# Three pairs of each output projection as seven products of quarters, with sums of the merged values

## The chip, the cores and the metric
The kernel runs on one core of a Trainium2 chip. The core has four compute engines with their own instruction queues: TensorE (PE, matmuls; PEld are its weight loads), VectorE (DVE), ScalarE (ACT) and GpSimd (POOL). SyncE (SP) and POOL issue most DMA transfers. Each queue runs in its own fixed order, and an instruction that waits for a semaphore holds up all that stand behind it. The metric is device microseconds of one execution, as a median of several.

## The reference, cut to what matters
Two layers over 512 tokens of 1024 channels. Each layer normalizes x, projects it, runs three token mixers, merges their gated outputs and adds one output projection to the residual. A final RMSNorm follows.

```
for layer in range(2):
    ...
    merged = (sigmoid(ga) * (ya @ w_br_a[layer])
              + sigmoid(gb) * (yb @ w_br_b[layer])
              + sigmoid(gc) * (yc @ w_br_c[layer]))
    x = x + merged @ w_out[layer]
return rmsnorm(x, final_norm_g)
```

All is float32. The kernel keeps that precision by splitting each operand into a high part (rounded to the matmul's format, `fp32r`) and a low part (the rest), and by three matmuls for each product: high x high, high x low, low x high (`mm3`, lines 130 to 132).

## The kernel before, in words
Channels lie on partitions, so x is eight tiles of 128 x 512 (channels x tokens). T0 and T1 are the first and the last 256 tokens. An output projection has eight units of 128 output channels. A unit reads two weight blocks of 128 x 512 (four blocks of 128 input channels each) and all eight merged tiles, high and low (`st["MH", i]`, `st["ML", i]`).

**Layer 0** (`o_item`, line 769 on): 24 matmuls of 512 columns per unit, then VectorE adds the residual out of PSUM (L782), SP stores the new x to DRAM (`x1d`), ScalarE and VectorE split it for layer 1 (L156, L159), and the squares are summed on POOL. After each unit one `v_item` of layer 1 runs (12 matmuls of 512 columns).

**Layer 1** (`last_item`, line 801 on): the units run twice, once for T0 and once for T1, 24 matmuls of 256 columns each, so that the final norm of the first half can be computed and stored while the second half is multiplied. VectorE adds the residual (L821) and sums squares (L832); ScalarE squares and scales.

**Weights.** `load` issues the transfers ahead of use, and `split_to` makes the high and low parts. Most blocks go the DMA way: POOL loads the block into the high place, ScalarE writes its negative (L1139), and POOL loads the block once more on top of it, adding (L1140). Blocks of layer 1's output projection go the raw way: SP loads them, ScalarE casts the high part (L1133), VectorE or POOL subtracts (L1135).

**The gates.** The merge gates of most units are already computed in pairs by `pair_steps`: a product of two units, seen as two by two quarters (unit x half of the input channels, against tokens T0 and T1), takes seven products of quarters instead of eight. Three of the seven weight operands are blocks as they are (forms 0, 1, 4); four are differences of blocks (forms 2, 3, 5, 6; L1119), made on VectorE from raw blocks. The token sides are the inputs themselves or four sums per pair of input blocks (`sums`, L603 to L611; `sum_places` names the tiles that keep them).

**What sets the order.** In layer 0 a scheduler orders the instructions of each queue; `urgent` raises a priority. From the last gate pair of layer 1 on the program is under `manual_schedule`: each queue has the order in which the code is written. Either way the order is fixed before the run. PSUM has banks of the kinds `mm` (3), `att` (4) and `pv` (1).

Of the kernel before, what the change touches and what calls it, by code (L numbers as in the profile page):

```python
# [13 lines left out]
P = 128  # L14
# [50 lines left out]
def tile_trunk(ctx: ExitStack, tc: tile.TileContext, xT, wpk, gT, gfT, bfg, snk,  # L65
# [21 lines left out]
    def pv_bank():  # L87
        return PS("pv", 1)
# [73 lines left out]
    def square_sum(x, k):  # L162
        if k == 0:
            st["acc"] = T([P, S], F32, "ys", 2)
            nc.scalar.activation(st["acc"], x, AF.Square)
        else:
            sq = tmp()
            nc.scalar.activation(sq, x, AF.Square)
            eng = nc.vector if k == KT - 1 else nc.gpsimd
            eng.tensor_tensor(st["acc"], st["acc"], sq, op=ALU.add)  # L170

    def rms_pe(_, tbs=range(4), accs=("acc",)):
        ps = st["ss"] = pv_bank()
# [423 lines left out]
    def sums(l, k):  # L597
        def run():
            a, b = st["xa", k], st["xa", k + 4]
            for kk, t in ((k, a), (k + 4, b)):  # L600
                nc.scalar.activation(t, t, AF.Copy, scale=g_sb[:, l, kk:kk + 1])
            u, v = tmp(), tmp()
            nc.vector.tensor_tensor(u[:, T0], a[:, T1], b[:, T1], op=ALU.add)  # L603
            nc.vector.tensor_tensor(u[:, T1], u[:, T0], a[:, T0], op=ALU.subtract)
            nc.vector.tensor_tensor(v[:, T0], a[:, T0], a[:, T1], op=ALU.subtract)
            nc.vector.tensor_tensor(v[:, T1], b[:, T0], u[:, T1], op=ALU.subtract)
            h, lo = sum_places(k)
            for n, w in ((0, u), (1, v)):
                c = slice(n * S, n * S + S)
                nc.scalar.copy(h[:, c], w)  # L610
                nc.vector.tensor_tensor(lo[:, c], w, rd(h[:, c]), op=ALU.subtract)  # L611
            st["SH", k], st["SL", k] = h, lo
        return run

# [31 lines left out]
    def pair_steps(l, br, i, last=False):  # L646
# [5 lines left out]

        def A(half, tok):
            return lambda k: (XH[k + 4 * half][:, tok], XL[k + 4 * half][:, tok])

        def Sm(m):
            c = slice((m - 1) * HT, m * HT)
            return lambda k: (st["SH", k][:, c], st["SL", k][:, c])

        def prod(bank, form, xf):  # L660
            def pe(HL):
                new = bank not in d
                if new:
                    d[bank] = att_bank()[:, :HT]
                wh, wl = HL[0]
                for k in range(4):
                    c = slice(k * P, (k + 1) * P)
                    xh, xl = xf(k)
                    mm3(d[bank], wh[:, c], wl[:, c], xh, xl, new and k == 0, k == 3,
                        bank != "c")  # L670
            step(pe, [("w", l, br, i, form)])
# [77 lines left out]
        prod("b", 2, Sm(1))  # L749
        do(now(e5))  # L750
        prod("a", 3, Sm(2))
# [4 lines left out]
        prod("b", 4, Sm(4))  # L756
        do(now(c12))
        prod("a", 5, Sm(3))
# [12 lines left out]
    def o_item(e):  # L771
        d = {}

        def pe(HL):
            if e == 0:
                load_res(0)
                load_res(1)
            d["ps"] = run_unit(HL, [st["MH", i] for i in range(8)], [st["ML", i] for i in range(8)], LATE)

        def post():  # L780
            x1 = tmp()
            nc.vector.tensor_tensor(x1, d["ps"], st["xr", e], op=ALU.add)  # L782
            if e + 2 < 8:
                load_res(e + 2)
            nc.sync.dma_start(x1d[:, e, :], x1)
            split_x(x1, 1, e)
            square_sum(x1, e)
        step(pe, [("o", 0, e, h) for h in range(2)])
        do(post)

    def load_half(n):
        hf, e = divmod(n, 8)
        t = st["xr", n] = T([P, S], F32, "sz", 2)[:, :HT]
        nc.sync.dma_start(t, x1d[:, e, hf * HT:(hf + 1) * HT])

    def last_item(hf, e):
        d = {}
        n = 8 * hf + e  # L800
        tok = slice(hf * HT, (hf + 1) * HT)

        def pe(HL):
            if n == 0:
                load_half(0)
                load_half(1)
            if hf == 0:
                st["WO", e] = HL
            ps = mm_bank()[:, :HT]
            for k in LATE:  # L810
                wh, wl = st["WO", e][k // 4]
                c = (k % 4) * P
                mm3(ps, wh[:, c:c + P], wl[:, c:c + P], st["MH", k][:, tok], st["ML", k][:, tok],
                    k == LATE[0], k == LATE[-1])
            d["ps"] = ps

        def post():
            if hf == 0:
                st["X2", e] = T([P, S], F32, "mg", 8)
            x2 = st["X2", e][:, tok]  # L820
            nc.vector.tensor_tensor(x2, d["ps"], st["xr", n], op=ALU.add)  # L821
            if n + 2 < 16:
                load_half(n + 2)
            acc = f"acc{hf}"
            if e == 0:
                st[acc] = T([P, S], F32, "ys", 2)[:, :HT]
                nc.scalar.activation(st[acc], x2, AF.Square)
            else:
                sq = tmp()[:, :HT]
                nc.scalar.activation(sq, x2, AF.Square)  # L830
                if e < KT - 1:
                    nc.vector.tensor_tensor(st[acc], st[acc], sq, op=ALU.add)  # L832
                else:
                    st[f"sq{hf}"] = sq
            nc.scalar.activation(x2, x2, AF.Copy, scale=st["gf"][:, e:e + 1])
        step(pe, [("o", L - 1, e, h) for h in range(2)] if hf == 0 else ())
        do(post)

# [15 lines left out]
    def last_projection():  # L854
        h0, h1 = range(0, 2), range(2, 4)
        for e in range(8):
            last_item(0, e)
            if e == 6:
                do(root_warm)
        for e in range(8):  # L860
            last_item(1, e)
            if e == 1:
                step(lambda _: rms_pe(_, h0, ("acc0", "sq0")))
                do(lambda: rms_root(h0))
            if e == 3:
                step(lambda _: rbc_pe(_, h0))
                do(lambda: store_half(0))
        step(lambda _: rms_pe(_, h1, ("acc1", "sq1")))
        do(lambda: rms_root(h1))
        step(lambda _: rbc_pe(_, h1))  # L870
        do(lambda: store_half(1))
# [9 lines left out]
    def layer(l):  # L881
# [140 lines left out]
        if l + 1 < L:  # L1022
            o_item(0)
            for e in range(1, 8):
                o_item(e)
                v_item(1, e - 1)
            v_item(1, 7)
        else:
            last_projection()
# [14 lines left out]
    PAIRS = [k[2:4] for k in seq if k[0] == "w" and k[1] == 0 and k[4] == 0]  # L1044

    def is_plain(key):
        return key[:2] in (("v", 0), ("f", 0), LAST_O)
# [5 lines left out]
    def quarters(key):  # L1053
        _, l, br, u, _ = key
        c = [COL["g" + "abc"[br]] + P * (u + w) for w in range(2)]
        return dict(B11=("u", l, c[0], 0), B12=("u", l, c[1], 0), B22=("u", l, c[1], 1), B21=("u", l, c[0], 1))

    def raw_slots(key):

        if key[0] == "w":  # L1060
            n = PAIRS.index(key[2:4])
# [6 lines left out]
        if key[0] == "f":  # L1068
            return [f"y{(8 + key[2]) % 10}"], None
        n = (2 * key[2] + key[3]) % 8  # L1070
        return [f"xh{n}" if n < 4 else f"xl{n - 4}"], ("w", key[1], 2, 6, 0)
# [6 lines left out]
    def places(key):  # L1078

        n = 2 * key[2] + key[3] if key[:2] == LAST_O else 0  # L1080
        h = T([P, CH], F32R, "wh", RINGH) if n < 10 else None
        if n < RING:
            return h, None
        if n < 10:
            return h, T([P, S], F32R, f"va{n - 7}")
        t = T([P, 2 * S], F32R, f"vb{n - 10}") if n < 14 else T([P, 1280], F32R, "P", 2)
        return t[:, :S], t[:, S:2 * S]

    def load(n):

        while ptr["load"] < min(n, len(seq)):
            i = ptr["load"]
            key = seq[i]
            if is_plain(key) or key[0] == "w" and key[4] == 0:
# [4 lines left out]
                for tag, (name, k) in zip(tags, src.items()):  # L1099
# [4 lines left out]
                    busy[tag] = i if name is None else i + 8  # L1104
                    nc.sync.dma_start(t[:, :w], ap)
            hl[i] = places(key)
            if not is_plain(key) and not (key[0] == "w" and key[4] in (2, 3, 5, 6)):
# [5 lines left out]
    def source(key):  # L1113
# [3 lines left out]
        b11, b12, b21, b22 = (raw[key[:4], n][:, :S] for n in ("B11", "B12", "B21", "B22"))  # L1117
        a, b, o = {2: (b12, b11, b11), 3: (b22, b11, b11), 5: (b22, b12, b12), 6: (b21, b11, b21)}[key[4]]
# [3 lines left out]
    def split_to(n):  # L1122
        while ptr["split"] < min(n, ptr["load"]):
# [6 lines left out]
            if is_plain(key) or key[0] == "w" and key[4] in (2, 3, 5, 6):  # L1130
# [3 lines left out]
                eng = nc.gpsimd if key[:2] == LAST_O and key[3] == 0 else nc.vector  # L1134
                eng.tensor_tensor(lo[:, :w], r[:, :w], rd(h[:, :w]), op=ALU.subtract)  # L1135
# [140 lines left out]
```

## Time and profile before

| | us |
|---|---|
| median of 3 runs (882.39 to 884.85) | 882.39 |
| the profiled execution's own time | 884.22 |
| its span | 882.5 |
| TensorE busy | 865.5 |
| VectorE busy | 567.9 |
| ScalarE busy | 510.4 |
| POOL busy | 440.5 |

The span is the stretch that the profiler saw, 1.7 us shorter than the execution's own time. Layer 0's output projection lies at about 392 to 460 us of the span, layer 1's at 822 to 870. Durations of neighbouring matmuls overlap, since they are pipelined: their pace is read from start to start.

### The profile page before, as it was taken

How to read it: one execution, taken by the hardware profiler on the slowest of the kernel's cores; microseconds unless marked ns; L12 is line 12 of the kernel's file. 1: busy time of each engine (PE TensorE's matmuls, PEld its weight loads, DVE VectorE, ACT ScalarE, POOL GpSimd, SP SyncE). 2: the span in 40 equal slices, each digit the busy share in tenths (PEclk: the TensorE clock that was granted, in tenths of full speed). 3: DMA queues.
4: the chain of work that ended last, by engine and by line, in shares of the span. 5: the costliest groups of instructions: out<-in, count | busy, mean ns of one | idle time of the engine just before them, and what ended most of it. 6: DMA issues, size and time to landing. Idle time of an engine off the chain costs nothing.

```text
span 882.5 us, 14401 instructions
## 1 busy us (share of the span) xinstructions
PE 865.5 (98%) x4866; PEld 750.1 (85%) x4866; DVE 567.9 (64%) x1242; ACT 510.4 (58%) x1072; POOL 440.5 (50%) x570
## 2 busy tenths in 40 slices
PE   9999999999999999999999999999999999999995
PEld 6988888888888889987888888888888888999994
DVE  7446788577576767752124658967685858687633
ACT  7477567565655655554335856666465756556541
POOL 5354576655444254566654446666444434544301
PEclk9999999999999999999999999999999999999997
DMA  9697768978989799999997886888899897998413
GB/s 303 142 207 141 161 142 168 190 144 189 199 182 228 193 185 247 205 200 284 250 233 156 174 164 149 153 168 172 158 205 193 186 223 158 226 247 183 160 48 111
DMA packets 97082, 163.83 MB, mean 186 GB/s; under 512 B 12144, under 2 KB 26864, under 8 KB 97008
## 3 DMA queue, kind: packets, MB, share of 16 engines
q0 software_dynamic: 71424, 121.70, 69.2%
q1 hardware_dynamic: 25440, 41.20, 14.2%
q8 instruction: 38, 0.62, 0.3%
q14 instruction: 36, 0.29, 0.1%
q10 hardware_dynamic: 144, 0.01, 0.0%
HBM read 153.43 MB, written 4.19 MB: 179 GB/s over the span
## 4 chain that ended last, share of the span: by engine, by line
PE 76%; issue 7%; POOL 5%; DMA 5%; DVE 3%; ACT 2%; SPq 0%; POOLq 0%; DVEq 0%; ACTq 0%
PE mm L131 17%; PE mm L130 17%; PE mm L132 17%; PE att L130 3%; PE att L131 3%; PE att L132 3%; PE pv L549 3%; PE att L503 3%; POOL wl L1140 3%; POOL wh L1110 2%; PE att L439 2%; PE att L438 2%; PE att L234 1%; PE att L235 1%; PE att L233 1%
## 5 line engine op out<-in xcount | busy, mean ns | idle before, releaser
L1140 POOL DMA_DIRECT2D wl<-in_wpk_dram x248 | 224.7, 925 | 185.8 <-ACT wl L1139 157.0
L1110 POOL DMA_DIRECT2D wh<-in_wpk_dram x248 | 169.6, 693 | 175.4 <-PE mm L132 130.2
L1139 ACT ACTIVATE wl<-wh 128x512 fp32r<-128x512 f32 (+3 forms) x248 | 148.3, 602 | 141.7 <-PE mm L132 113.2
L130 PE MATMUL mm<-xh,wh 128*128 128x512 f32 x544 | 217.6, 400 | 0.0
L131 PE MATMUL mm<-xl,wh 128*128 128x512 f32 x544 | 214.5, 394 | 0.0
L132 PE MATMUL mm<-xh,wl 128*128 128x512 f32 x544 | 214.4, 394 | 0.0
L132 PEld LDWEIGHTS mm<-xh,wl 128*128 128x128 f32 x544 | 102.2, 188 | 24.1
L130 PEld LDWEIGHTS mm<-xh,wh 128*128 128x128 f32 x544 | 102.3, 188 | 22.2
L131 PEld LDWEIGHTS mm<-xl,wh 128*128 128x128 f32 x544 | 102.3, 188 | 22.1
L474 ACT ACTIVATE P<-P,ng 128x256 f32<-128x256 f32 (+3 forms) x128 | 67.0, 525 | 24.9 <-DVE ng L472 24.4
L130 PE MATMUL mm<-y,wh 128*128 128x512 f32 (+1 forms) x132 | 49.9, 378 | 1.2 <-ACT y L711 1.2
L529 DVE TENSOR_TENSOR PL<-att,PH 128x512 fp32r<-128x512 f32 (+2 forms) x84 | 46.1, 598 | 7.0 <-ACT PH L528 7.0
L131 PE MATMUL mm<-y,wh 128*128 128x512 f32 (+1 forms) x132 | 50.1, 379 | 0.3 <-DVE y L712 0.3
L132 PE MATMUL mm<-y,wl 128*128 128x512 f32 (+1 forms) x124 | 47.5, 383 | 0.0
L130 PE MATMUL att<-xh,wh 128*128 128x256 f32 x144 | 40.7, 282 | 0.0
L492 DVE TENSOR_SCALAR P<-P,den 128x256 f32<-128x256 f32 (+3 forms) x128 | 39.8, 376 | 1.0
L132 PE MATMUL att<-xh,wl 128*128 128x256 f32 x144 | 40.4, 281 | 0.0
L131 PE MATMUL att<-xl,wh 128*128 128x256 f32 x144 | 40.4, 281 | 0.0
L528 ACT CAST PH<-att 128x512 fp32r<-128x512 f32 (+2 forms) x84 | 38.8, 526 | 1.3 <-PE att L503 0.6
L439 PE MATMUL att<-qk,qk 128*128 128x256 f32 (+2 forms) x128 | 36.9, 308 | 0.0
L503 PE MATMUL att<-ident,P 128*128 128x128 f32 x284 | 36.2, 272 | 0.0
L438 PE MATMUL att<-qk,qk 128*128 128x256 f32 (+2 forms) x128 | 36.1, 308 | 0.0
(260 smaller groups left out, 2034.8 us busy)
## 6 DMA issues: line engine op xcount, KB each, us to landing
wh<-in_wpk_dram POOLq DMA_DIRECT2D x196, 256.0 KB, 4.7
wl<-in_wpk_dram POOLq DMA_DIRECT2D x196, 256.0 KB, 5.2
y<-in_wpk_dram SPq DMA_DIRECT2D x32, 256.0 KB, 5.5
qk<-in_wpk_dram SPq DMA_DIRECT2D x24, 256.0 KB, 4.8
wh<-in_wpk_dram POOLq DMA_DIRECT2D x32, 192.0 KB, 5.0
wl<-in_wpk_dram POOLq DMA_DIRECT2D x32, 192.0 KB, 4.4
tmp<-tmp SPq DMA_DIRECT2D x80, 64.0 KB, 4.0
mg<-in_xT_dram SPq DMA_DIRECT2D x8, 256.0 KB, 5.7
```

The costliest lines, as they stand in the source:

```text
L130: nc.tensor.matmul(ps, wh, xh, start=first, stop=False, skip_group_check=part)
L131: nc.tensor.matmul(ps, wh, xl, start=False, stop=False, skip_group_check=part)
L132: nc.tensor.matmul(ps, wl, xh, start=False, stop=last, skip_group_check=part)
L438: nc.tensor.matmul(ps, q[:, qs], kh[:, a:a + n], start=True, stop=False)
L439: nc.tensor.matmul(ps, q2[:, qs], k2[:, a:a + n], start=False, stop=True)
L474: nc.scalar.activation(pb, pb, AF.Exp, bias=ng[:, i:i + 1], scale=-1.0, accum_out=den[:, i:i + 1])
L492: nc.vector.tensor_scalar(blks[i], blks[i], den[:, i:i + 1], None, op0=ALU.mult)
L503: nc.tensor.transpose(ps[:, c * P:(c + 1) * P], pt[:, src * P:(src + 1) * P], st["ident"])
L529: nc.vector.tensor_tensor(st["PL"][:, o:o + n], bk[:, :n], rd(hh), op=ALU.subtract)
L1110: nc.gpsimd.dma_start(hl[i][0][:, :w], ap)
L1139: nc.scalar.activation(lo[:, :w], rd(h[:, :w]), AF.Copy, scale=-1.0)
L1140: nc.gpsimd.dma_start(lo[:, :w], ap, accum_op=ALU.add)
```

## The change
Each output projection keeps two plain units (0 and 1 in layer 0, 6 and 7 in layer 1). The six others form three pairs, `o_pair`, each with seven products of 12 matmuls of 256 columns in place of two units. The token sides are the merged tiles or four sums of them (`sums_m`, four groups: tiles k and k + 4). The weight operands are made like those of the gates. In layer 0 all seven of a pair go the raw way; in layer 1 the four differences do, and the three plain blocks go the DMA way. The two plain units of layer 1 now go the DMA way too. The raw blocks of a pair go into the places `va0` to `va3` or `y0` to `y3`. The squares of layer 0's projection are summed on VectorE, not on POOL. The residuals of layer 1 are loaded at the start of its projection into the places of the split x.

```
+    def sums_m(k):
+        return lambda: four_sums(k, st["M", k], st["M", k + 4])
...
+    def o_pair(l, e, bank, res, finish):
+        d = {}
+        prod = products(("w", l, 3, e), d, bank)
...
+        def add(u, tok, b, first):
+            def run():
...
+                other = st["xr", e + u] if first else x[u]
+                nc.vector.tensor_tensor(x[u][:, tok], d[b], other[:, tok], op=ALU.add)
+                if (not first) or (u, tok) == (0, T1):
+                    finish(e + u, x[u], tok)
+            return urgent(run) if l + 1 < L else run
+        res(e)
+        prod("a", 0, M(0, T0))
+        do(add(0, T0, "a", True))
+        prod("b", 2, sum_part(1))
+        do(add(1, T1, "b", True))
+        prod("a", 3, sum_part(2))
+        do(add(1, T0, "a", True))
+        prod("c", 1, M(1, T0))
+        do(add(0, T0, "c", False))
+        prod("a", 5, sum_part(3))
+        do(add(1, T1, "a", False))
+        prod("b", 4, sum_part(4))
+        do(add(1, T0, "b", False))
+        prod("a", 6, M(1, T1))
+        do(add(0, T1, "a", True))
...
+    def first_projection():
...
+        do(lambda: load_res(0), lambda: load_res(1), sums_m(0))
+        o_item(0)
+        do(sums_m(1))
+        o_item(1)
+        do(sums_m(2), sums_m(3))
+        o_pair(0, 2, mm_bank, res, finish)
+        v_item(1, 0)
+        v_item(1, 1)
+        o_pair(0, 4, mm_bank, res, finish)
...
     def last_projection():
...
+        do(residuals, sums_m(0), sums_m(1))
+        last_item(T0, 6)
+        do(root_warm, sums_m(2))
+        last_item(T0, 7)
+        do(sums_m(3))
+        for e in (0, 2, 4):
+            o_pair(1, e, att_bank, lambda e: None, finish)
+        step(lambda _: rms_pe(_, h0, ("acc0", "sq0")))
+        do(lambda: rms_root(h0))
+        last_item(T1, 6)
+        step(lambda _: rbc_pe(_, h0))
+        do(lambda: store_half(0))
+        last_item(T1, 7)
...
     def raw_slots(key):
         if key[0] == "w":
-            n = PAIRS.index(key[2:4])
+            if key[2] == 3:
+                odd = (key[3] // 2 + key[1]) % 2 == 0
+                return [f"y{m}" if odd else f"va{m}" for m in range(4)], ("p", key[1], 2, 7)
```

The order of the queues shows what the words leave out. First piece: VectorE's queue at the end of layer 1's last gate pair. Before, after the seventh merged tile's low part (`y<-mg,y`, 512 wide) came one weight split, the last gate's four rows and the first add of a unit:

```order
L712 TENSOR_TENSOR y_1758_8952<-mg_7539,y_1757_8951 128x512
L1135 TENSOR_TENSOR wl_8971<-xl_1746_8904,wh_8906 128x512
L742 TENSOR_TENSOR tmp_8805<-att_8783,rbc_5113 128x256
L699 SCALAR_TENSOR_TENSOR tmp_8805<-tmp_8805,mm_8869 128x256
L700 TENSOR_TENSOR mg_7256<-mg_7256,tmp_8805 128x256
L712 TENSOR_TENSOR y_1745_8889<-mg_7256,y_1744_8888 128x256
L821 TENSOR_TENSOR mg_9016<-mm_8984,sz_8980 128x256
```

In the changed kernel:

```order
L726 TENSOR_TENSOR y_1800_9181<-mg_7771,y_1799_9180 128x512
L1201 TENSOR_TENSOR va_1790_9161<-va_1791_9163,va_1790_9161 128x512
L1216 TENSOR_TENSOR wl_9197<-va_1790_9161,wh_9171 128x512
L756 TENSOR_TENSOR tmp_9037<-att_9015,rbc_5345 128x256
L713 SCALAR_TENSOR_TENSOR tmp_9037<-tmp_9037,mm_9100 128x256
L714 TENSOR_TENSOR mg_7488<-mg_7488,tmp_9037 128x256
L726 TENSOR_TENSOR y_1788_9116<-mg_7488,y_1787_9115 128x256
L607 TENSOR_TENSOR tmp_9223<-mg_6473,mg_7230 128x256
```

The first pair's first weight difference (`va`) and its split now stand ahead of the last gate's rows, and the four groups of sums (L607 to L615) stand behind them.

Second piece: VectorE's queue inside the projection of layer 1. Before, a unit is an add, a sum of squares and a weight split:

```order
L821 TENSOR_TENSOR mg_9058<-mm_9023,sz_8982 128x256
L832 TENSOR_TENSOR ys_9020<-ys_9020,tmp_9062 128x256
L1135 TENSOR_TENSOR va_1768_9012<-xh_1766_9009,wh_9011 128x512
L821 TENSOR_TENSOR mg_9101<-mm_9066,sz_9018 128x256
L832 TENSOR_TENSOR ys_9020<-ys_9020,tmp_9105 128x256
L1135 TENSOR_TENSOR vb_1777_9053<-xh_1776_9051,vb_1777_9053 128x512
```

In the changed kernel, the first pair's adds (L816, `att` is the bank of a product) have the next pair's differences (L1201) and splits (L1216) between them:

```order
L816 TENSOR_TENSOR mg_9380<-att_9358,xh_1805_9211 128x256
L816 TENSOR_TENSOR mg_9400<-att_9382,xh_1806_9213 128x256
L1201 TENSOR_TENSOR y_1830_9323<-y_1831_9325,y_1830_9323 128x512
L1216 TENSOR_TENSOR wl_9415<-y_1830_9323,wh_9371 128x512
L816 TENSOR_TENSOR mg_9400<-att_9358,xh_1806_9213 128x256
L1201 TENSOR_TENSOR y_1830_9323<-y_1832_9327,y_1830_9323 128x512
L1216 TENSOR_TENSOR wl_9435<-y_1830_9323,wh_9372 128x512
L816 TENSOR_TENSOR mg_9380<-att_9420,mg_9380 128x256
L886 TENSOR_TENSOR ys_9280<-ys_9280,tmp_9440 128x256
L816 TENSOR_TENSOR mg_9400<-att_9358,mg_9400 128x256
L1201 TENSOR_TENSOR y_1831_9325<-y_1832_9327,y_1831_9325 128x512
```

Each difference is followed at once by the split that needs ScalarE's cast of it.

Third piece: VectorE's queue at the start of layer 0's projection. Before, the last two merged tiles are finished and the adds of the units follow:

```order
L712 TENSOR_TENSOR y_872_4385<-mg_2983,y_871_4384 128x512
L699 SCALAR_TENSOR_TENSOR tmp_4246<-tmp_4246,mm_4307 128x256
L700 TENSOR_TENSOR mg_2700<-mg_2700,tmp_4246 128x256
L712 TENSOR_TENSOR y_863_4326<-mg_2700,y_862_4325 128x256
L782 TENSOR_TENSOR tmp_4445<-mm_4415,sz_4411 128x512
```

In the changed kernel:

```order
L726 TENSOR_TENSOR y_876_4389<-mg_2983,y_875_4388 128x512
L713 SCALAR_TENSOR_TENSOR tmp_4246<-tmp_4246,mm_4307 128x256
L1216 TENSOR_TENSOR wl_4383<-va_866_4371,wh_4379 128x512
L714 TENSOR_TENSOR mg_2700<-mg_2700,tmp_4246 128x256
L1201 TENSOR_TENSOR va_866_4371<-va_867_4373,va_866_4371 128x512
L726 TENSOR_TENSOR y_862_4324<-mg_2700,y_861_4323 128x256
L1201 TENSOR_TENSOR va_867_4373<-va_868_4375,va_867_4373 128x512
L1216 TENSOR_TENSOR wl_4405<-va_866_4371,wh_4380 128x512
L793 TENSOR_TENSOR tmp_4461<-mm_4431,sz_4415 128x512
```

A split (`wl<-va`) and a difference of the first pair's weights now stand between the rows of the last merged tile (`y<-mg,y`, 256 wide), and more of them behind it.

## Rows read from the trace of the kernel before

**Rows 1.** the page's busy times and shares of the engines
```profile
PE 865.5 (98%) x4866; PEld 750.1 (85%) x4866; DVE 567.9 (64%) x1242; ACT 510.4 (58%) x1072; POOL 440.5 (50%) x570
```

**Rows 2.** TensorE's timeline: start us, us, line, tiles out<-in, shape [idle before <-releaser]
```profile
390.06 0.40 PE L132 MATMUL mm<-va,wl 128*128 128x512 f32 x1
390.29 0.28 PE L130 MATMUL att<-xh,wh 128*128 128x256 f32 x1
...
391.71 0.39 PE L130 MATMUL mm<-qk,wh 128*128 128x512 f32 x1
...
397.93 0.50 PE L131 MATMUL mm<-y,wh 128*128 128x512 f32 x1
...
398.50 0.39 PE L130 MATMUL mm<-qk,wh 128*128 128x512 f32 x1
...
404.06 0.39 PE L233 MATMUL att<-wh,xh 128*128 128x512 f32 x1
...
820.26 0.40 PE L132 MATMUL mm<-va,wl 128*128 128x512 f32 x1
...
822.05 0.28 PE L130 MATMUL mm<-qk,wh 128*128 128x256 f32 x1
...
825.71 0.38 PE L131 MATMUL mm<-y,wh 128*128 128x256 f32 x1 [0.34 <-DVE y L712]
```

**Rows 3.** VectorE's timeline, last projection, adds of two half units
```profile
849.28 0.42 DVE L821 TENSOR_TENSOR mg<-mm,sz 128x256 f32<-128x256 f32 x1 [2.40 <-PE mm L132]
852.13 0.42 DVE L821 TENSOR_TENSOR mg<-mm,sz 128x256 f32<-128x256 f32 x1 [2.43 <-PE mm L132]
```

**Rows 4.** VectorE's timeline, one group of four sums and what follows
```profile
728.25 0.42 DVE L603 TENSOR_TENSOR tmp<-tmp,tmp 128x256 f32<-128x256 f32 x1
...
731.23 0.68 DVE L632 TENSOR_TENSOR tmp<-mm,rbc 128x512 f32<-128x512 f32 x1
731.83 0.68 DVE L1135 TENSOR_TENSOR wl<-qk,wh 128x512 fp32r<-128x512 f32 x1
```

**Rows 5.** VectorE's timeline, a weight difference and its split
```profile
812.36 0.69 DVE L1119 TENSOR_TENSOR y<-y,y 128x512 f32<-128x512 f32 x1
813.78 0.69 DVE L1135 TENSOR_TENSOR wl<-y,wh 128x512 fp32r<-128x512 f32 x1 [0.74 <-ACT wh L1133]
```

**Rows 6.** VectorE's timeline, an add and the sum of squares behind it
```profile
836.46 0.42 DVE L821 TENSOR_TENSOR mg<-mm,sz 128x256 f32<-128x256 f32 x1
837.37 0.64 DVE L832 TENSOR_TENSOR ys<-ys,tmp 128x256 f32<-128x256 f32 x1 [0.48 <-ACT tmp L830]
```

**Rows 7.** DMA issues: out<-in, engine, op, count, KB each, median us to landing
```profile
y<-in_wpk_dram SPq DMA_DIRECT2D x32, 256.0 KB, 5.5
...
xh<-in_wpk_dram SPq DMA_DIRECT2D x8, 256.0 KB, 4.3
```

**Rows 8.** VectorE's timeline, adds of merged tiles, and the last gate
```profile
822.61 1.67 DVE L700 TENSOR_TENSOR mg<-mg,tmp 128x512 f32<-128x512 f32 x1
...
826.17 0.42 DVE L742 TENSOR_TENSOR tmp<-att,rbc 128x256 f32<-128x256 f32 x1
...
828.42 0.43 DVE L712 TENSOR_TENSOR y<-mg,y 128x256 fp32r<-128x256 f32 x1 [0.47 <-ACT y L711]
828.77 0.42 DVE L821 TENSOR_TENSOR mg<-mm,sz 128x256 f32<-128x256 f32 x1
```

**Rows 9.** ScalarE's timeline, the table load
```profile
845.05 1.28 ACT L212 ACT_TABLE_LOAD   x1
```

**Rows 10.** TensorE's timeline, the first matmul after the last unit
```profile
870.03 0.28 PE L176 MATMUL pv<-ones,ys 128*128 128x1 f32 x2
```

**Rows 11.** two stretches after it: busy, count, granted clock, DMA share, GB/s
```profile
870.00:872.00 2.00, 1.14 (x10) 0.97 (x8) 0.42 (x1) 0.92 (x2) 0.00 (x0) 1.00 0.00 0
872.00:874.00 2.00, 0.66 (x2) 0.29 (x2) 0.71 (x5) 0.26 (x1) 0.00 (x0) 0.53 0.00 0
```

**Rows 12.** POOL's timeline, a subtraction beside VectorE's add at 822.61
```profile
822.44 1.29 POOL L1135 TENSOR_TENSOR wl<-xl,wh 128x512 fp32r<-128x512 f32 x1 [2.86 <-ACT wh L1133]
```

More of the change, by code (lines that the diff above doesn't have):

```diff
@@ L168, in square_sum, with rms_pe @@
             nc.scalar.activation(sq, x, AF.Square)
[L169 removed]
+            eng = nc.vector if k == KT - 1 else side
             eng.tensor_tensor(st["acc"], st["acc"], sq, op=ALU.add)
[L172 to L173 removed]
+    def rms_pe(_, tbs=range(4), accs=("acc",), bank=pv_bank):
+        ps = st["ss"] = bank()
         for n, tb in enumerate(tbs):
@@ L651, in pair_steps @@
         now = urgent if br == 2 else (lambda fn: fn)
+        prod = products(("w", l, br, i), d, att_bank)
         def A(half, tok):
[L654 to L671, printed above, removed]
+            return part(XH, XL, half, tok)
         def branch(u):
@@ new lines, in quarter @@
+    def quarter(e, x, tok, last):
+        hf = int(tok == T1)
+        x2 = x[:, tok]
+        acc = f"acc{hf}"
+        if acc not in st:
+            st[acc] = T([P, S], F32, "ys", 2)[:, :HT]
+            nc.scalar.activation(st[acc], x2, AF.Square)
+        else:
+            sq = tmp()[:, :HT]
+            nc.scalar.activation(sq, x2, AF.Square)
+            if last:
+                st[f"sq{hf}"] = sq
+            else:
+                nc.vector.tensor_tensor(st[acc], st[acc], sq, op=ALU.add)
+        nc.scalar.activation(x2, x2, AF.Copy, scale=st["gf"][:, e:e + 1])
@@ L817, in post @@
         def post():
-            if hf == 0:
+            if tok == T0:
                 st["X2", e] = T([P, S], F32, "mg", 8)
[L820 to L836, printed above, removed]
+            x2 = st["X2", e]
+            nc.vector.tensor_tensor(x2[:, tok], d["ps"], st["xr", e][:, tok], op=ALU.add)
+            quarter(e, x2, tok, e == 7 and tok == T1)
+        step(pe, [("o", L - 1, e, h) for h in range(2)] if tok == T0 else ())
         do(post)
@@ L855, in last_projection, with residuals, finish @@
         h0, h1 = range(0, 2), range(2, 4)
[L856 to L868, printed above, removed]
+        def residuals():
+            for n, e in enumerate((6, 7, 0, 1, 2, 3, 4, 5)):
+                t = st["xr", e] = T([P, S], F32, f"xh{4 + n}" if n < 4 else f"xl{n}")
+                nc.sync.dma_start(t, x1d[:, e, :])
+        def finish(e, x, tok):
+            quarter(e, x, tok, e == 5 and tok == T0)
+        do(residuals, sums_m(0), sums_m(1))
[11 more added lines that the diff above has]
+        last_item(T1, 7)
+        step(lambda _: rms_pe(_, h1, ("acc1", "sq1"), att_bank))
         do(lambda: rms_root(h1))
@@ L1022, in layer @@
         if l + 1 < L:
[L1023 to L1027, printed above, removed]
+            first_projection()
         else:
```

138 lines of the change are left out of this document (85 added, 53 removed).

## The prediction
> **What bounds the kernel now.** I read the page's engine shares first, then TensorE's timeline and waits, then VectorE's and ScalarE's timelines around the two output projections. TensorE is busy 865.5 of 882.5 us [rows 1], and its matmuls follow each other without gaps: nothing else sets the time except short waits for the last merged tiles, as at 825.71 [rows 2]. One unit of layer 0's projection (24 matmuls of 512 columns) takes 404.06 - 398.50 = 5.56 us; one product of quarters (12 matmuls of 256 columns) takes 391.71 - 390.29 = 1.42 us [rows 2]. In layer 1 one unit's half (24 matmuls of 256) takes 852.13 - 849.28 = 2.85 us [rows 3].
>
> **What the change removes.** A pair of units becomes seven products, 7 x 1.42 = 9.94 us. Before, a pair cost 2 x 5.56 = 11.12 us in layer 0 and 4 x 2.85 = 11.40 us in layer 1. Three pairs each save 3 x 1.18 = 3.5 us and 3 x 1.46 = 4.4 us, 7.9 us in all, if TensorE never waits. A second small saving: POOL no longer subtracts during the last projection.
>
> **What it adds, on VectorE.** Per pair four weight differences with four splits (512 columns, 0.60 us apart when nothing holds them [rows 4]), seven adds out of PSUM and four sums of squares; before the pairs, four groups of sums. VectorE runs its rows in the order shown above, and most of the new rows wait for a ScalarE cast in between, so the price of a chain is more than its busy time:
> - Difference, cast, split: 813.78 - 812.36 = 1.42 us to the split, 2.0 us with it [rows 5].
> - One group of four sums: 731.23 - 728.25 = 2.98 us; its first split is over 0.6 us before that [rows 4].
> - An add and the sum of squares behind it: 837.37 - 836.46 = 0.91 us until the second starts [rows 6].
>
> **Layer 1, step by step** (times on the profiled execution's axis).
> 1. The first pair's four raw blocks go into places that the last branch product still reads; it ends at 820.26 + 0.40 = 820.66 [rows 2]. So their loads can be issued only then. Loads of this size from SP landed after 4.3 and 5.5 us in the median [rows 7]; with 4.9, and 0.45 for the second issue, both operands of the first difference are there at 826.0.
> 2. That difference and its split stand on VectorE ahead of the last gate's work (first piece of the order). They end at 828.1; the last gate's four rows take 828.77 - 826.17 = 2.6 us [rows 8] and end at 830.7, 1.9 us later than before.
> 3. Then the sums: 3 x 2.98 for three groups; between the second and third a difference with its split and one add (2.0 + 0.4); between the third and fourth another (2.0), an add and a sum of squares (1.3), and a table load of 1.28 us [rows 9], which now stands on ScalarE ahead of the third group's casts; then 2.3 for the fourth group up to its first split. 830.7 + 8.9 + 2.4 + 1.3 + 3.3 + 2.3 = 848.9; I carry 849.2 for the hops between engines.
> 4. TensorE arrives much earlier. The first half unit starts at 822.05 and, with the wait for the seventh merged tile that the trace shows up to 825.71, ends near 826.7 [rows 2]; one more half unit and one product bring it to 831.0. The second product reads the four groups in turn: it can end at 849.5, not at 832.4. That is 17.1 us of TensorE idle, but for nine short matmuls.
> 5. The third product accumulates in the bank of the first, so it waits until VectorE has added the first one out. That add stands behind the second split of the fourth group and one more difference (0.6 + 2.0): 852.3 instead of 849.5.
> 6. From there VectorE sets the pace, since the next pair's weights are made between the adds (second piece of the order). Per pair: 4 x 2.0 for weights, about 7 x 0.36 for adds, 4 x 0.9 for sums of squares, 14.2 us, where TensorE needs 9.94. Two pairs bring the third pair's third product to 880.7. That pair has no further weights to make: five products (7.1), four tiny matmuls, two half units with a transpose between (6.2) end at 894.1.
> 7. From TensorE's last unit to the end 882.5 - 870.03 = 12.4 us stay [rows 10]: 906.5, that is +24.0.
>
> **Layer 0.** The raw blocks wait for the same reason until 390.06 + 0.40 [rows 2] and stand third in SP's queue, so they land at 396.1 to 396.7. The first weight split, which waits for them and for a cast, stands ahead of the last merged tile's last split (third piece of the order): that tile is ready at 399.4 instead of 397.93 [rows 2], +1.5 us; with loads that are as fast as TensorE would need this is -0.5, with slow ones +2.2. From 399.4 to the third group's first split VectorE has 13 rows of 0.60 to 0.70 us, three of 0.6 and ten of 256 columns at 0.35 to 0.45 [rows 4, 8]: 13.6 us, 413.0, where TensorE arrives at 400.0 + 5.6 + 3.5 + 0.9 = 410.0. It waits 3.0 us there and 2.0 us on the fourth group and the bank adds behind it. The later two pairs have plain projection steps of the next layer between them (5.5 us per pair), and VectorE keeps up. Sum: +1.5 + 5.0 - 3.5 = +3.0; bounds -3.5 (all hidden) and +6.
>
> **Sum.** 882.5 + 3.0 + 24.0 = 909.5 us of span, 911.2 us as a time like the 884.22 us of the profiled execution. That execution lies 1.8 us above the median of 882.39, so 909.4 against the median. While TensorE idles in step 4 its granted clock will not stay up: after the last dense matmuls at 870.03 it was 1.00 until 872 and 0.53 in the next 2 us [rows 10, 11]. The first products behind the gap then run slower; I add 1.5 us, between nothing (VectorE hides it) and 1.42 us for each product at the lower level. Forecast: 911 us.
>
> The Trainium skill's page "TensorE: Matmul & The Clock Gate", Part 1, says that the default is half rate and that only sustained work lifts it to 2.4 GHz. The drop in rows 11 agrees. By that rule alone every gap of three or four us between this kernel's products would cost again, which is the second rival. The Trainium skill's page "SBUF — State Buffer", section "SBUF: two separate sides", says that GpSimd and a VectorE operation with two SBUF inputs exclude each other on a port. The add at 822.61 that took 1.67 us, beside POOL's of 1.29 us, where 512 columns of two tiles take 0.69 [rows 5], agrees [rows 8, 12]. POOL's subtractions are gone now, so by the rule that microsecond comes back; it only shortens VectorE's way to step 2, where the load is later anyway.
>
> **Rivals.**
> - TensorE keeps the pace after the first wait: the casts come early enough that VectorE's pair costs no more than 9.94 us. VectorE's busy time per pair alone, about 8 x 0.6 + 11 x 0.36 = 8.8 us, speaks for it; the strict order of difference, cast, split against it. It saves 2 x 4.2 us: 902 us.
> - The lower clock: in every gap of 3 to 4 us of step 6 the granted clock falls, and products take up to 2.8 us. VectorE's adds then wait for products: some 2 to 3 us a pair, 918 us.
> - The other side, faster: TensorE alone sets the time and VectorE's new work is hidden, as its share of 64% might suggest [rows 1]. The place is the wait in step 4. It decides at 832: if the fourth group's first split is done there and not at 849, the kernel gains up to 7.9 us, 874.5. Against it: four groups take 11.9 us after 828.8 even without the weights between them, 840.
> - A floor for the forecast's mechanism: VectorE's busy time alone, with no wait for ScalarE at all, from 826.0 to the third pair is 36 us (32 rows of 512 columns at 0.60, some 45 of 256 at 0.36) and would end the span at 888.4 instead of 906.5; with layer 0's gain whole, 885.
>
> **How the numbers follow.** The forecast with its pace by VectorE 70%; TensorE's pace after the wait 12%; the lower clock in every gap 11%; something between the floor and 895 us 2%; hidden 5%, of which 1% ends within 0.3%, about what a measurement of this kernel can tell from no change. So faster 0.04, same 0.01, slower 0.95. The range 896 to 922 takes in the first two rivals and the bounds of layer 0 and of the loads; it leaves out the floor, the hidden case and a clock that is low throughout.
>
> **What would show it.** Right: in the last projection TensorE idle for about 17 us on VectorE's split of the fourth sums; the third product of each pair released by an add; pairs 13 to 15 us apart; a lower granted clock in that stretch; a wait of about 3 us in layer 0's first pair. Wrong: the second product of layer 1's first pair starting before 835 us (plus layer 0's shift), pairs 10 us apart, or the raw blocks landing before 823.

## The result, and the profile after

The changed kernel takes 915.88 us in the median of 4 runs (913.34 to 916.12), against 882.39 us (4 runs, 882.13 to 884.85). The ratio, of the means of all runs, is 1.0367 with a 95% interval of 1.0341 to 1.0392: slower by 32.4 us, while the two medians lie 33.5 us apart. The forecast was 911 us with a range of 896 to 922. The profiled execution took 915.93 us, its span is 914.2 us. The page's busy line, as in [rows 1]:

```profile
PE 870.1 (95%) x4938; PEld 758.2 (83%) x4938; DVE 627.7 (69%) x1369; ACT 528.7 (58%) x1106; POOL 425.8 (47%) x558
```

TensorE is busy 4.6 us longer over a span that is 31.7 us longer, so 27.1 us of the loss is TensorE standing still. Two sums of its waits between 815 and 905 us (engine, tile, line <- releaser: us in total, times, longest):

```profile
PE att L130 <- DVE mg L816: 8.7, 4, 3.4
PE att L176 <- ACT tmp L882: 1.5, 1, 1.5
```

Here mg L816 are the adds out of PSUM. TensorE's timeline has the long waits in order of time, for [rows 2, 3], with the rows between them left out; the last number is the idle time and its releaser. PH and P are the sums of groups 2 and 3, y L725 is the cast of the seventh merged tile:

```profile
829.89 0.58 PE L130 MATMUL mm<-y,xh 128*128 128x256 f32 x1 [4.37 <-ACT y L725]
839.60 0.39 PE L130 MATMUL att<-vb,wh 128*128 128x256 f32 x1 [1.28 <-ACT vb L614]
846.30 0.58 PE L130 MATMUL att<-PH,wh 128*128 128x256 f32 x1 [5.47 <-ACT PH L614]
852.35 0.58 PE L130 MATMUL att<-P,wh 128*128 128x256 f32 x1 [4.53 <-ACT P L614]
856.01 0.58 PE L130 MATMUL att<-vb,wh 128*128 128x256 f32 x1 [2.13 <-DVE mg L816]
870.45 0.36 PE L130 MATMUL att<-vb,wh 128*128 128x256 f32 x1 [2.79 <-DVE mg L816]
884.64 0.55 PE L130 MATMUL att<-vb,wh 128*128 128x256 f32 x1 [3.42 <-DVE mg L816]
901.00 0.28 PE L176 MATMUL att<-ones,ys 128*128 128x1 f32 x2
```

The rows at 856.01, 870.45 and 884.64 are the third products of the three pairs: 14.44 and 14.19 us apart, where seven products need 9.94. VectorE's side of it, grouped by line between 818 and 895 us (busy, mean ns | idle before and what ended it):

```profile
L1216 DVE TENSOR_TENSOR wl<-va,wh 128x512 fp32r<-128x512 f32 x8 | 5.5, 693 | 5.6 <-ACT wh L1215 5.6
L886 DVE TENSOR_TENSOR ys<-ys,tmp 128x256 f32<-128x256 f32 x10 | 4.3, 425 | 5.2 <-ACT tmp L882 5.2
L1216 DVE TENSOR_TENSOR wl<-y,wh 128x512 fp32r<-128x512 f32 x4 | 2.8, 693 | 3.2 <-ACT wh L1215 3.2
```

In this stretch VectorE stood 14.0 us before its own splits and sums of squares, each time for a ScalarE cast or square that had just been asked for. The late seventh tile is seen on ScalarE and on VectorE (ScalarE's rows first; of VectorE's some are left out):

```profile
821.18 0.63 ACT L706 ACTIVATE tmp<-tmp 128x512 f32<-128x512 f32 x1 [1.62 <-DVE tmp L700]
828.70 0.63 ACT L1220 ACTIVATE wl<-wh 128x512 fp32r<-128x512 f32 x1 [6.89 <-DMA wh<-in_wpk_dram]
829.24 0.60 ACT L725 CAST y<-mg 128x512 fp32r<-128x512 f32 x1
```

```profile
822.83 0.69 DVE L714 TENSOR_TENSOR mg<-mg,tmp 128x512 f32<-128x512 f32 x1
829.87 0.69 DVE L726 TENSOR_TENSOR y<-mg,y 128x512 fp32r<-128x512 f32 x1 [6.35 <-ACT y L725]
830.48 0.69 DVE L1201 TENSOR_TENSOR va<-va,va 128x512 f32<-128x512 f32 x1
831.91 0.69 DVE L1216 TENSOR_TENSOR wl<-va,wh 128x512 fp32r<-128x512 f32 x1 [0.74 <-ACT wh L1215]
...
834.77 0.43 DVE L726 TENSOR_TENSOR y<-mg,y 128x256 fp32r<-128x256 f32 x1 [0.47 <-ACT y L725]
```

The tile was merged at 823.5 (L714), no later than in before [rows 8]. Its cast stood on ScalarE behind a negation that belongs to the first pair's weights and waited 6.89 us for a load. The raw blocks of the first difference (L1201 at 830.48) were late as well. SP issued them from 821.33 on; the last number of the second line is the median time from issue to landing:

```profile
821.33 2.25 SPq L1185 DMA_DIRECT2D va<-in_wpk_dram  x4
va<-in_wpk_dram SPq DMA_DIRECT2D x4, 256.0 KB, 7.8
```

The difference needs the first two of them. The second was issued at 821.71 and landed 7.8 us later, at 829.5; so even without the held cast the difference could have started only 1.0 us earlier. The clock, in stretches (busy of PE, PEld, DVE, ACT, POOL; then the granted clock, DMA share, GB/s):

```profile
830.00:840.00 10.00, 8.56 (x46) 7.79 (x46) 8.06 (x18) 3.75 (x7) 1.60 (x3) 0.73 1.08 358
840.00:850.00 10.00, 1.88 (x5) 1.08 (x5) 6.88 (x15) 5.44 (x11) 0.88 (x1) 0.61 0.13 40
850.00:856.00 6.00, 1.38 (x3) 0.79 (x3) 4.84 (x11) 3.77 (x7) 1.72 (x3) 0.50 0.31 42
856.00:860.00 4.00, 3.99 (x21) 4.00 (x22) 2.60 (x5) 0.62 (x1) 1.14 (x2) 0.59 1.02 280
860.00:870.00 10.00, 7.66 (x65) 7.45 (x63) 5.93 (x13) 6.82 (x14) 2.83 (x4) 1.00 0.71 158
```

In layer 0 TensorE's waits between 380 and 500 us are these; before had one of 0.5 us:

```profile
PE mm L130 <- ACT y L725: 1.7, 1, 1.7
PE mm L130 <- ACT PH L614: 1.4, 1, 1.4
PE mm L130 <- DVE tmp L816: 0.6, 1, 0.6
PE mm L131 <- DVE PL L615: 0.6, 1, 0.6
```

### The profile page after: what moved, and what is told of

It is laid out like the page before. It is cut to its first block, busy times and chain, and to the rows that moved or that the text cites. A ratio compares the mean times of both kernels' runs of the same rounds, so it can differ in the third digit from the quotient of the medians.

```text
span 914.2 us, 14706 instructions
## 1 busy us (share of the span) xinstructions
PE 870.1 (95%) x4938; PEld 758.2 (83%) x4938; DVE 627.7 (69%) x1369; ACT 528.7 (58%) x1106; POOL 425.8 (47%) x558
## 3 DMA queue, kind: packets, MB, share of 16 engines
q1 hardware_dynamic: 25440, 43.30, 14.3%
## 4 chain that ended last, share of the span: by engine, by line
PE 84%; DVE 7%; DMA 4%; ACT 3%; issue 1%; SPq 0%; DVEq 0%; ACTq 0%
PE mm L130 18%; PE mm L131 17%; PE mm L132 17%; PE att L130 5%; PE att L131 5%; PE att L132 5%; PE pv L549 4%; PE att L503 3%; PE att L439 2%; PE att L438 2%; DMA va<-in_wpk_dram 1%; PE att L234 1%; PE att L235 1%; PE att L233 1%; DVE wl L1216 1%
## 5 line engine op out<-in xcount | busy, mean ns | idle before, releaser
L1221 POOL DMA_DIRECT2D wl<-in_wpk_dram x245 | 222.0, 928 | 263.2 <-ACT wl L1220 234.1
L1220 ACT ACTIVATE wl<-wh 128x512 fp32r<-128x512 f32 (+3 forms) x245 | 145.8, 601 | 120.7 <-PE mm L132 85.2
L1215 ACT CAST wh<-y 128x512 fp32r<-128x512 f32 (+1 forms) x46 | 27.8, 617 | 32.1 <-DVE y L1201 23.1
L130 PE MATMUL att<-vb,wh 128*128 128x256 f32 x120 | 34.8, 290 | 10.4 <-DVE mg L816 8.3
L130 PE MATMUL mm<-y,wh 128*128 128x512 f32 (+1 forms) x112 | 42.8, 382 | 1.7 <-ACT y L725 1.7
L131 PE MATMUL mm<-y,wh 128*128 128x512 f32 (+1 forms) x112 | 42.9, 383 | 0.0
L132 PE MATMUL mm<-y,wl 128*128 128x512 f32 (+1 forms) x112 | 42.8, 382 | 0.0
L1216 DVE TENSOR_TENSOR wl<-y,wh 128x512 fp32r<-128x512 f32 (+1 forms) x47 | 34.9, 753 | 10.6 <-ACT wl L1220 5.1
```

The lines of the kernel that those rows point to most:

```text
L130: nc.tensor.matmul(ps, wh, xh, start=first, stop=False, skip_group_check=part)
L131: nc.tensor.matmul(ps, wh, xl, start=False, stop=False, skip_group_check=part)
L132: nc.tensor.matmul(ps, wl, xh, start=False, stop=last, skip_group_check=part)
L1216: nc.vector.tensor_tensor(lo[:, :w], r[:, :w], rd(h[:, :w]), op=ALU.subtract)
L1220: nc.scalar.activation(lo[:, :w], rd(h[:, :w]), AF.Copy, scale=-1.0)
L1221: nc.gpsimd.dma_start(lo[:, :w], ap, accum_op=ALU.add)
```

## The experiments

The theory: in layer 1 VectorE's and ScalarE's queues, which run in program order, set the time; the sums come too late for the second product, and the weights between the adds hold the pairs to 14 us. The rivals: the lower clock; landing times of loads; another price of the short products. Losses below are ratios to before times 882.4 us; the changed kernel's own is +32.4.

**One layer at a time.** Edits: layer 1's last projection, weight places and loads as in the old kernel; or the same for layer 0.

> Layer 0's projection as in the changed kernel, layer 1's as before. Theory (VectorE's order in layer 1's last projection makes the loss): the trace after shows layer 1's last gate pair 0.1 us earlier than before, so this is 882.3, within 880.5 to 884.5. Rival (layer 0 pays its predicted +3.0): 885.4. Rival (the saving of three pairs comes through whole): 878.9.

> Layer 0's projection as before, layer 1's as in the changed kernel. Theory: the whole loss, 882.4 + 33.6 = 916, within 913.5 to 917.5, with the same waits of the second product. Rival (layer 0's changed order upsets the loads of layer 1): at most 905.

Layer 0 alone: 886.31 us, ratio 1.0036 (1.0024 to 1.0049), +3.2. Layer 1 alone: 911.18 us, 1.0322 (1.0308 to 1.0337), +28.4. The sum, 31.6, is the whole loss within the intervals. Layer 1 alone ended below the theory's 913.5, layer 0 alone above its 884.5, for one reason. On layer 0 the theory's number was wrong and the rival's, the prediction's +3.0, right. The 0.1 us from which I had argued came from one execution: at layer 0's last gate pair it was 2.3 us ahead of before (a row at 384.93 against 387.26), and the late-residuals kernel below, whose VectorE and TensorE run the same rows in the same order, has that row at 387.27. A span's earlier stretches scatter by that much between executions. From this row to the end of layer 0's projection the cost is 2.2 to 5.4 us in nine executions with the new layer 0, 2.8 in the changed kernel's.

**What the sums and what the weights cost.** Edits, in layer 1 only:

```
- do(residuals, sums_m(0), sums_m(1))        # and sums_m(2), sums_m(3)
+ do(residuals)                              # products read MH, ML
...
+ if key[1:3] == (1, 3): return raw block    # no difference
+ hl[i] = (h, None)                          # low part: a zero tile
```

> Layer 1's pairs read halves of the merged tiles where the sums stood; the sixteen additions, eight casts and eight splits of the sums in layer 1 are left out. Theory: the second product's waits of 1.3, 5.5 and 4.5 us go and the first add comes earlier, the third product starts near 842 instead of 856.0; the later pairs stay 14.0 to 14.6 us apart: 902, within 899 to 906. Rival (the raw blocks and the casts behind them set the start): no more than 6 us gained, 910.

> Layer 1's pairs multiply with raw blocks instead of their differences and with a zero low part: VectorE loses twelve differences and twelve splits; TensorE's and ScalarE's work is the same. Theory: three pairs of such rows stood ahead of the first add (about 6 us), so the third product starts near 848; and the pairs then come at TensorE's 10 to 11 us instead of 14.3, -7 us: 900, within 896 to 904. Rival (the pace of the pairs is made by the lower clock and the adds, not by the weights): pairs stay over 13 us apart, 908.

Without sums: 905.57 us, 1.0265 (1.0251 to 1.0280), +23.4. Without differences: 899.81 us, 1.0189 (1.0174 to 1.0205), +16.7. Both theories' ranges held, both rivals fell. One kernel leaves out the sums, the other the differences and their low parts. TensorE's timeline without sums (rows between left out):

```profile
832.50 0.58 PE L130 MATMUL mm<-y,xh 128*128 128x256 f32 x1 [4.56 <-ACT y L728]
848.12 0.55 PE L130 MATMUL att<-qk,wh 128*128 128x256 f32 x1 [6.11 <-DVE mg L819]
876.86 0.36 PE L130 MATMUL att<-qk,wh 128*128 128x256 f32 x1 [3.45 <-DVE mg L819]
```

From the seventh tile to the third product it takes 15.6 us instead of 26.1; two pairs still take 28.7 us, 14.4 each. The third product was expected near 842; this execution has its seventh tile 2.6 us later than the changed kernel's, so it is still 3.5 us late. Without differences the same way takes 18.1 us:

```profile
833.12 0.58 PE L130 MATMUL mm<-y,xh 128*128 128x256 f32 x1 [3.49 <-ACT y L725]
851.21 0.58 PE L130 MATMUL att<-vb,wh 128*128 128x256 f32 x1 [0.15 <-DVE mg L816]
```

From there TensorE does not wait in any pair (columns as above):

```profile
860.00:870.00 10.00, 10.00 (x87) 10.00 (x86) 4.68 (x11) 7.35 (x17) 4.04 (x6) 1.00 0.81 159
870.00:880.00 10.00, 10.00 (x87) 10.00 (x86) 4.68 (x11) 4.75 (x11) 0.86 (x1) 1.00 0.41 52
```

So the sums are 10.5 us of the first wait, the weights ahead of the first add 8.0, and the weights alone make the pairs' pace. These do not tell whether VectorE's work or its order costs.

**Same work, other order.** Edit: a weight split is put off until the add behind it has been issued, a sum of squares until the next add.

```
- nc.vector.tensor_tensor(lo, r, rd(h), op=ALU.subtract)
+ pend.append(low)          # flushed at the next step
- nc.vector.tensor_tensor(st[acc], st[acc], sq, op=ALU.add)
+ later.append(...)         # flushed behind the next add
```

> The changed kernel, with layer 1's weight splits put behind the add that follows and each sum of squares behind the next add: same instructions, other order on VectorE. Theory (VectorE is slow because it stands behind ScalarE's casts and squares, 0.69 and 0.48 us at a time, four of each per pair): pairs 10.5 to 12 us apart instead of 14.3, third product near 854: 908, within 905 to 911. Rival (VectorE's busy time sets the pace): pairs stay at 14 or over, 915.

904.33 us, 1.0249 (1.0227 to 1.0271), +22.0: 10.4 us less with the same instructions, and just below the expected range of 905 to 911. After the third product (852.23) TensorE waits once more in the pairs, 0.96 us, for a load:

```profile
860.00:870.00 10.00, 9.04 (x76) 8.84 (x75) 7.22 (x15) 6.06 (x14) 3.82 (x6) 1.00 0.82 158
870.00:880.00 10.00, 10.00 (x87) 10.00 (x86) 7.14 (x17) 5.85 (x14) 1.72 (x2) 1.00 0.43 71
```

VectorE is busier (7.1 of 10 us) and TensorE full. The pace of 14.3 us was waiting in order, not work.

**The late seventh tile, the early sums, the clock.** Edits: residual loads 1 to 7 issued later in the program; groups 0 and 1 of the sums around the seventh merge; 84 matmuls that nothing reads, in TensorE's waits.

```
- do(residuals, sums_m(0), sums_m(1))
+ do(lambda: residuals(0, 1), sums_m(0), sums_m(1))      # e6
...
+ if last and l + 1 == L: do(sums_m(0))                  # e7
  branch(1)
  do(now(merge(1, slice(0, S))))
+ if last and l + 1 == L: do(sums_m(1))
...
+ filler(key, form, k)                                   # e8
```

> The changed kernel, with seven of the eight residual loads issued after the third group of sums and later instead of right behind the raw blocks. Theory (the cast of the seventh merged tile stands on ScalarE behind a negation that waits for a weight load, and that load landed after 8.4 us because the residuals shared the DMA engines): the load lands 2 to 3 us earlier, TensorE's wait of 4.4 us before the first half unit falls under 2.5, all behind it moves: 913. Rival (the load is late in its own queue, behind the raw blocks): no change, 916.

> The changed kernel, with the sums of groups 0 and 1 issued during the last gate pair, before and behind the seventh tile's merge, where VectorE sat idle over 8 us. Theory (the sums' place in VectorE's order makes the 17 us wait): two groups of 2.9 us leave the chain, third product near 850: 910, within 908 to 912. Rival (they push the last merged tiles back by as much): 916.

> The changed kernel with 84 idle matmuls of 512 columns on TensorE, put into its waits of layer 1's projection, so that the granted clock has less reason to fall; nothing else reads them. Theory (the clock counts only behind the last wait, where the last pair's five products took 9.6 us instead of 7.1): 2 to 3 us, 913. Rival (the low clock of the whole stretch makes the loss): first products of 1.42 instead of 2.6 us everywhere, 906 or less.

e6: 916.65 us, 1.0395 (1.0376 to 1.0415). No gain, and no test either: SP does not stand in VectorE's order, so three of the loads went out 2.1 us behind the raw blocks (2.3 in the changed kernel) and only four moved. These had gone out from 828.13 on in the changed kernel, when the negation's load was all but there. The negation's load took 7.2 us (issued 821.22, used 828.47) instead of 8.3 (820.41, 828.70). How much the residuals cost it, and the raw blocks, stays open.

e7: 912.83 us, 1.0343 (1.0323 to 1.0362), which overlaps the changed kernel's interval. VectorE's rows show why it is half of what I expected (rows between left out): the merge ends with the split that waits for the cast, so group 1 (the second L607) stood behind that wait too, and ahead of the last gate's rows.

```profile
822.20 0.42 DVE L607 TENSOR_TENSOR tmp<-mg,mg 128x256 f32<-128x256 f32 x1
825.76 0.69 DVE L714 TENSOR_TENSOR mg<-mg,tmp 128x512 f32<-128x512 f32 x1
831.31 0.69 DVE L726 TENSOR_TENSOR y<-mg,y 128x512 fp32r<-128x512 f32 x1 [4.86 <-ACT y L725]
831.92 0.42 DVE L607 TENSOR_TENSOR tmp<-mg,mg 128x256 f32<-128x256 f32 x1
836.79 0.42 DVE L756 TENSOR_TENSOR tmp<-att,rbc 128x256 f32<-128x256 f32 x1
```

From the last gate pair's row L700 (821.59, against 820.40) the third product comes 33.0 us later instead of 35.6: one group, 2.6, left the chain, not two.

e8: 913.37 us, 1.0355 (1.0332 to 1.0379); by time alone it is not told from the changed kernel. Its trace tells more (the clock in two stretches, then the seventh tile and the three third products):

```profile
840.00:850.00 10.00, 10.00 (x55) 8.66 (x55) 6.90 (x15) 6.17 (x11) 0.88 (x1) 1.00 0.22 83
850.00:860.00 10.00, 8.21 (x48) 6.58 (x47) 8.04 (x17) 4.47 (x8) 2.86 (x4) 1.00 0.61 113
```

```profile
830.68 0.58 PE L130 MATMUL mm<-y,xh 128*128 128x256 f32 x1 [3.41 <-ACT y L737]
856.81 0.38 PE L130 MATMUL att<-vb,wh 128*128 128x256 f32 x1 [0.80 <-DVE mg L828]
870.44 0.36 PE L130 MATMUL att<-vb,wh 128*128 128x256 f32 x1 [0.48 <-DVE mg L828]
884.64 0.36 PE L130 MATMUL att<-vb,wh 128*128 128x256 f32 x1 [0.71 <-DVE mg L828]
```

The granted clock stays at 1.00. This execution reached its seventh tile 0.79 us later; from there to the third product it takes 26.13 us, as without the matmuls (26.12): VectorE sets it. The pairs are 13.63 and 14.20 us apart, against 14.44 and 14.19. In the changed kernel's first pair one add (858.97) waited 0.71 us for a product at the lower clock, which fits the 0.8 us; one execution each doesn't tell it from scatter. Behind the last wait it pays: from 884.64 to the sums of squares' matmuls 7.1 us (891.78) instead of 9.6 (894.21). In these two executions the clock costs 2.4 us there and at most 0.8 before; the rival's 10 are refuted. The Trainium skill's page "TensorE: Matmul & The Clock Gate", Part 1, says that the full rate has to be earned by activity; this run agrees, since matmuls without any use kept it at 1.00 in a stretch where it had been 0.61 and 0.50.

**Mended versions.** Edits: e9, layer 0 only, the first pair's raw loads tied to the seventh merged tile and two projection steps moved ahead; e10, e5's order, weight splits behind the last merged tiles, sums 0 and 1 behind the seventh tile; e11, both, with two pairs in layer 1; e12, layer 0 only, four plain units, then two pairs. In e10 and e11 the low part of one difference per first pair is taken from a block already overwritten; instructions and sizes are those of the others.

```
+ nc.vector.tensor_copy(t[:, :1], rd(st["ML", 6][:, S - 1:S]))       # e9, e11
...
+ if not (chunks and chunks[0] in HOLD): split_to(pos + RING)        # e10, e11
...
+ full_item(4); full_item(5); o_pair(1, 0, ...); o_pair(1, 2, ...)   # e11
...
+ o_item(0) ... o_item(3); o_pair(0, 4, ...); o_pair(0, 6, ...)      # e12
```

> Layer 1's projection as before; layer 0's pairs as changed, with two edits: the first pair's raw loads wait for the seventh merged tile's split (a copy of one column ahead of them), and two projection steps of the next layer stand ahead of the first pair instead of behind it. Theory (layer 0 pays 1.2 to 2.7 us for the first weight split ahead of that tile, 2.6 for the sums and under 2 for the clock behind these waits, and saves 3.5): all three waits go and the saving stays, 879.3, within 878 to 881. Rival (seven short products have some other price): no better than 882.

> The changed kernel, in layer 1: the order of e5_reorder, the weight splits that ScalarE and VectorE had ahead of the last two merged tiles put behind them, and the sums of groups 0 and 1 directly behind the seventh tile. Theory: TensorE's wait of 4 us for the seventh tile goes, and the third product starts 7 to 9 us earlier than e5's 852.2: 896, within 893 to 899. Rival (the first pair's weights land no earlier, and TensorE waits for them instead): 901 to 904.

> Both ideas, with two pairs instead of three in layer 1: units 6 and 7 in halves and units 4 and 5 whole stand ahead of the pairs, 17 us of plain products over the sums; layer 0 as in e9_layer0_mended; four of the residual loads wait for the third group of sums; the table load stands behind the first pair. Theory: no wait for sums or adds, two savings of 1.46 us and layer 0's 3: 877.5, within 875.5 to 880.5. Rival (the weights of units 4 and 5 land late, since 250 to 360 GB/s already flow there): 882 or more.

> Layer 1's projection as before; in layer 0 four units stay plain and come first, with two projection steps of the next layer between them, and only units 4 to 7 go in pairs. Theory (a pair of layer 0 saves 1.18 us where its sums and weights are made under other products, and the costs of the changed kernel come from the first pair standing too near the last merged tiles): no wait for the sums, under 1 us for the last merged tile, 2 x 1.18 us saved: 880.1, within 878.5 to 881.5. Rival (the pairs cost VectorE's or ScalarE's time wherever they stand): 882.5 or more.

e9: 894.64 us, 1.0132 (1.0105 to 1.0158), +11.7: the theory's number fell, for a reason that neither side named. The wait for the last merged tiles is down to 0.7 us and that for the sums is gone, but TensorE now waits for other weights and for a cast of the unit just finished:

```profile
PE mm L261 <- DMA wl<-in_wpk_dram: 3.9, 3, 1.9
PE att L233 <- ACT xh L156: 3.3, 1, 3.3
PE att L234 <- DMA wl<-in_wpk_dram: 2.4, 1, 2.4
PE mm L130 <- ACT y L725: 0.7, 2, 0.5
```

By the kernel's code the loader goes through the blocks in one order and stops at the first whose place is not free, so holding the raw blocks back holds back every load behind them. That this made the waits is not shown: the moved projection steps stand in the same kernel, and no run has one edit without the other.

e10: 899.86 us, 1.0190 (1.0159 to 1.0220), +16.8, between the two forecasts. TensorE's wait for the seventh tile is gone, and the negation that was put off now releases its second load later (issued at 836.37, against 829.63 in the changed kernel):

```profile
843.22 0.58 PE L132 MATMUL att<-qk,wl 128*128 128x256 f32 x1 [11.07 <-DMA wl<-in_wpk_dram]
849.56 0.39 PE L130 MATMUL att<-vb,wh 128*128 128x256 f32 x1 [1.28 <-DVE mg L818]
```

e11: 903.53 us, 1.0235 (1.0209 to 1.0260): far from its theory's 877.5. The seventh tile of layer 1 is merged 9.3 us later than before (831.86 against 822.61); in e9's profiled execution, the slowest of its six, it is 15.4 us. From there on e11 loses 9.8 us more, 5.0 of them in one wait for the low weights of the plain units. e12: 888.91 us, 1.0062 (1.0041 to 1.0084), +5.5, where the theory had 880.1: no wait for sums beyond 0.3 us, but the tile waits (2.2) and two for weights (1.4, 1.2) cost more than 2 x 1.18. That a distance from the last merged tiles is enough is thus refuted; why the tiles still come late was not tested. No version tried beats the kernel before.

## Why the prediction was right, point by point

The direction and the mechanism were right, and the size lay in the range; it came that near with the help of errors of opposite sign. The span grew by 31.7 us, forecast were 27.0 and 1.5 for the clock.

- **What the pairs save** (3.5 and 4.4 us): nothing speaks against it, though no version tried shows it as a gain. Seven products without waits keep TensorE's pace of before, as e4's and e5's full stretches show.
- **Layer 0, +3.0**: the number was right, e1 measured +3.2 (2.1 to 4.3), but in part by luck. In the profiled execution it is 1.2 us more for the last merged tile (forecast 1.5) and 2.6 for sums and adds (forecast 5.0). Most of the rest is clock, which I had not put into this term: 0.97 on the mean from 395 to 460 us, where before has 1.00, by estimate 2.0 us.
- **Steps 1 and 2, gate rows done at 830.7**: mis-sized, 835.2 measured (0.2 us of it is where this execution stood). Two terms were too small. The raw blocks were to be there at 826.0; the second landed at 829.5, after 7.8 us where I had put 4.9, and it was issued 0.6 us later. That alone is 3.5 of the 4.5 us. And I had counted what stands ahead of the last gate's rows on VectorE and not what stands ahead of the seventh tile's cast on ScalarE: the negation of a plain weight block. It held the difference until 830.48, 1.0 us past the landing. With the negation moved, TensorE's wait for the seventh tile went (e10), but the raw blocks took as long (a median of 7.9 us). The add ahead of that tile took 0.69 us at 822.83, without POOL's subtraction beside it, and 1.67 before [rows 8, 12]; as forecast, nothing came of it.
- **Steps 3 to 5, third product at 852.3**: 856.01. The chain of sums, table load, differences and first add took 20.8 us from the gate rows on, where 21.6 were forecast, so it ended 3.7 us late; e3 and e4 show both of its parts. The waits fell elsewhere than said: of 17.1 us in the second product 11.6 came there, nearly all ended by ScalarE's casts of the sums (L614) and not by VectorE's split, and 4.4 earlier, at the seventh tile.
- **Step 6, pairs 14.2 us apart**: 14.44 and 14.19, and 14.4 to 15.6 in e2, e6 and e7. That it is the order and not the busy time was the first rival's question; e5 answers it. That rival, 902 us, was wrong for this kernel, and is 2 us from what the same instructions take in a better order.
- **Last pair to last unit, 13.4 us, and the tail, 12.4**: 16.4 and 13.2. The five products ran at the lower clock for their first 5.3 us (matmuls 0.21 us apart from 884.6 to 889.9, 0.12 behind) and took 9.6 instead of 7.1 us. The last sum of squares waits 1.48 us for ScalarE.
- **Clock, +1.5**: 2.4 by e8, behind the last wait, where nothing covers it and where I had not looked; I had put it behind the gap of step 4. There VectorE's pace hides all but at most 0.8 us, near the lower bound that I had named, and the second rival's 2 to 3 us in every pair did not come.

The tail from the seventh merge on thus cost 31.5 us where 25.5 were forecast. By the same rows e2 has 31.1, by its times 28.4: its tile was merged 3.5 us earlier than in before (819.08), and no run shows the cause. The profiled execution was 2.3 us ahead before the projections began, which the run of the same order shows to be scatter, and 0.3 more in between; so the sum came out 3.2 us short where the tail alone was 6.0 us short: that part of its nearness is luck.

## What to carry to other kernels

A cheaper product pays only if its operands can be made under other work: count what each in-order engine has between the last input and the first use, on ScalarE as well as on VectorE, and where each row asks another engine for something and then stands. Take the landing time of a load from a stretch in which as many others are under way: 7.8 us here, not 4.9. The same rows in an order that puts other work into these round trips gave back 10 of 32 us. An edit that moves one load must be followed through the queue that it stands in: with one negation put off, TensorE stood 11.07 us before its second load, and where raw loads were held back, TensorE waited for other weights.

## What the runs showed of the hardware

The granted clock fell to 0.61 and 0.50 in stretches where TensorE was busy 1.9 of 10 and 1.4 of 6 us; when dense work began again at 856.01, matmuls of 256 columns followed each other every 0.21 us until 859.2 and every 0.12 us from then on; at 884.64, behind a wait of only 3.42 us, it took until 889.9. A load of 256 KB that POOL issued at 820.41 was there after 8.3 us, and four that SP issued from 821.33 on after a median of 7.8, while the DMA engines moved 235 GB/s at a mean share of 0.98 (820 to 830 us). Before, between 815 and 835 us, loads of this size that SP issued took medians of 2.7 and 3.2 us at 155 GB/s and a share of 0.49. The Trainium skill's page "DMA: Bandwidth & Descriptors", section "Latency and other measured facts", says that access latency grows with load; the direction agrees, and these are the numbers here.
